# Seven products of quarter blocks for eight in the down projections of three feed-forward stages

## The chip, the cores and the metric

The kernel runs on one core of a Trainium2 chip. Its metric is the device time in microseconds (us) of one execution of the whole program, the median of three runs. A profiled execution is recorded besides, and every duration in this text comes from that one.

Five engines work side by side, each through its own queue of instructions in order: TensorE multiplies matrices (PE in the profile, its weight loads PEld), VectorE (DVE) and ScalarE (ACT) work element by element, GpSimd (POOL) too, and SyncE (SP) issues most transfers. An instruction starts when its predecessor on its engine lets it and when the semaphores it waits for have been raised by the others.

## The reference

The reference is a transformer block with a mixture of experts, followed by a second block of two layers. Each of these layers holds two feed-forward stages, four in all, which are the part that matters here:

```
D_MODEL = 1024; SEQ = 512; D_FF = 2816; FFN_HALF = 0.5

def swiglu(h, w_gate, w_up, w_down):
    return (jax.nn.silu(h @ w_gate) * (h @ w_up)) @ w_down

for i in range(DEPTH_2):                                   # 2 layers
    h = rmsnorm_2(x, ffn1_norm[i])
    x = x + FFN_HALF * swiglu(h, ffn1_w_gate[i], ffn1_w_up[i], ffn1_w_down[i])
    ...                                                    # layer 0: pooling mixer, layer 1: latent attention
    h = rmsnorm_2(x, ffn2_norm[i])
    x = x + FFN_HALF * swiglu(h, ffn2_w_gate[i], ffn2_w_up[i], ffn2_w_down[i])
```

In order of time: ffn1 of layer 0, pooling, ffn2 of layer 0, ffn1 of layer 1, attention, ffn2 of layer 1.

## The kernel before

All products are made in float32 by three passes. An operand is split into a high part (`hi`, rounded to the type fp32r in which TensorE multiplies at full rate) and the remainder (`lo` = operand - `hi`), and `mm3` (lines 246 to 249) adds hi·hi, hi·lo and lo·hi. ScalarE makes the high part with a cast, VectorE the remainder with a subtraction.

The residual stream `X` stays in SBUF: 512 tokens as 4 tiles of 128, 1024 features each. The normed input lies transposed in `xT`. The function `ffn` (line 1030) walks over the 22 blocks of 128 hidden features in three parts, `PARTS` (blocks 0 to 7, 8 to 14, 15 to 21). For each block it makes gate and up, 24 matmuls of 128x512 each, into one of two tiles `pA`; ScalarE takes Silu of the gate (L1052), VectorE multiplies by the up half (L1054), and the hidden block is split into `hh`, `hl` (L255, L256). At the end of a part comes its down projection, in two halves of 512 output features: four accumulators (2 `pB`, 2 `pC`, one for each token tile), and for each block 4 x 3 matmuls of 128x512. When an accumulator is done, VectorE adds half of it onto `X` (L1103).

The class `Weights` feeds the weights. A plan lists, in the order of their use, chunks of 1 MB (one DMA into one of 4 `wraw` tiles) and units (pieces of a chunk of up to 128x1024). `next()` hands out a split unit and lets the splitting run ahead by `look` = 2 units: ScalarE casts `whi` (L161) and VectorE subtracts to `wlo` (L162). There are `NU` = 4 buffers of `whi` and of `wlo`. A chunk's tile is free when its last unit is split, and then the next DMA is issued.

What order the instructions have in each queue is decided when the program is built, by a scheduler with its own estimate of readiness and by priorities (`tc.high_priority`); on the chip each queue then runs in that order.

Of the kernel before, what the change touches and what calls it, by code (L numbers as in the profile page):

```python
# [99 lines left out]
class Weights:  # L100
# [51 lines left out]
    def _split(self, i):  # L152
        c, pick, raw = self.units[i]
        src = pick(self.tiles[c])
# [36 lines left out]
def tile_net(ctx, tc, I, out):  # L191
# [195 lines left out]

    PARTS = [(0, 8), (8, 15), (15, 22)]

    def plan_ffn(which, i):  # L390
        g, u, d = (I[f"ffn{which}_w_{n}_2"][i] for n in ("gate", "up", "down"))
        for f0, f1 in PARTS:
# [643 lines left out]

    def ffn(pool, gain, last=False, hook=None, before=None):
        xT = pair()
# [7 lines left out]
        def proj(a, m, w, c0, c1):  # L1046
            for k in range(K):
                mm3(a[:, m * 512 + c0:m * 512 + c1], [x[:, k] for x in w], [x[:, k, c0:c1] for x in xT], k == 0, k == K - 1)

        def hidden_of(a, m, sl):  # L1050
# [4 lines left out]
            hh = pool.tile([P, S], F32R, name="hh", tag="hh", bufs=8)  # L1055
            hl = pool.tile([P, S], F32R, name="hl", tag="hl", bufs=8)
            split(hh, hl, sl)
            return hh, hl

        for f0, f1 in PARTS:  # L1060
            if hook is not None and f0 > 0:
# [412 lines left out]
    with tc.tile_pool(name="pmc", reuse_waits=RW, bufs=1) as pmc:  # L1474
        with tc.tile_pool(name="f10", reuse_waits=RW, bufs=1) as p_:
# [11 lines left out]
    with tc.tile_pool(name="ml", reuse_waits=RW, bufs=1) as ml:  # L1487
        with tc.tile_pool(name="f20", reuse_waits=RW, bufs=1) as p_:
# [37 lines left out]
```

## Time and profile before

| | |
|---|---|
| three runs, median (lowest to highest) | 2657.82 us (2657.05 to 2658.94) |
| profiled execution, its own time | 2660.51 us |
| span of that profile, first to last instruction | 2658.6 us |
| mean granted TensorE clock | 0.989 of full speed |
| instructions | 28917, of which 12006 matmuls |
| HBM read | 407.92 MB, 154 GB/s over the span |

How to read it: an engine's share of the span tells only the average. Which engine bounds a stage is read from that stage's window, and what a removed instruction is worth from the pace at which that engine issues. Matmuls are pipelined: the duration of one is longer than the distance to the next. The same holds to a smaller degree for VectorE, where an instruction may start a little before the one ahead of it has ended.

### The profile page before, as it was taken

How to read it: one execution, taken by the hardware profiler on the slowest of the kernel's cores; microseconds unless marked ns; L12 is line 12 of the kernel's file. 1: busy time of each engine (PE TensorE's matmuls, PEld its weight loads, DVE VectorE, ACT ScalarE, POOL GpSimd, SP SyncE). 2: the span in 40 equal slices, each digit the busy share in tenths (PEclk: the TensorE clock that was granted, in tenths of full speed). 3: DMA queues.
4: the chain of work that ended last, by engine and by line, in shares of the span. 5: the costliest groups of instructions: out<-in, count | busy, mean ns of one | idle time of the engine just before them, and what ended most of it. 6: DMA issues, size and time to landing. Idle time of an engine off the chain costs nothing.

```text
span 2658.6 us, 28917 instructions
## 1 busy us (share of the span) xinstructions
PE 2552.4 (96%) x12006; PEld 1856.7 (70%) x12006; DVE 1045.2 (39%) x1620; ACT 735.8 (28%) x1243; POOL 88.2 (3%) x142
## 2 busy tenths in 40 slices
PE   6999889999998999998999999999999999999999
PEld 4755644333335887888887878787779777888887
DVE  5655322222215333336333334333335666533332
ACT  4343210000003322224322223222224645322221
POOL 1000100000001000001000000000001000000000
PEclk9999899999998999999999999999999999999999
DMA  7255369999996222332222223223222111232321
GB/s 266 92 178 172 145 278 420 410 418 419 417 420 242 96 95 87 95 103 83 95 96 87 87 95 104 95 79 103 78 89 80 58 58 64 64 99 75 119 77 59
DMA packets 185493, 411.90 MB, mean 155 GB/s; under 512 B 7461, under 2 KB 126785, under 8 KB 157713
## 3 DMA queue, kind: packets, MB, share of 16 engines
q1 hardware_dynamic: 183168, 403.73, 41.6%
q10 hardware_dynamic: 1008, 3.34, 0.3%
q0 software_dynamic: 1184, 2.97, 0.3%
q8 instruction: 94, 1.54, 0.2%
q14 instruction: 39, 0.31, 0.0%
HBM read 407.92 MB, written 2.10 MB: 154 GB/s over the span
## 4 chain that ended last, share of the span: by engine, by line
PE 60%; issue 30%; DMA 3%; DVE 3%; ACT 3%; POOL 1%; SPq 0%; POOLq 0%; ACTq 0%; DVEq 0%
PE pA L968 9%; PE pA L247 7%; PE pA L248 7%; PE pA L249 7%; PE pB L968 4%; PE pC L249 3%; PE pC L248 3%; PE pC L247 3%; PE pB L248 2%; PE pB L249 2%; PE pB L247 2%; PE pC L942 1%; PE ms L1397 1%; PE pC L1015 1%; PE pC L741 1%
## 5 line engine op out<-in xcount | busy, mean ns | idle before, releaser
L161 ACT CAST whi<-wraw 128x1024 fp32r<-128x1024 f32 (+2 forms) x334 | 335.9, 1011 | 1093.7 <-PE pA L248 685.8
L162 DVE TENSOR_TENSOR wlo<-wraw,whi 128x1024 fp32r<-128x1024 f32 (+2 forms) x334 | 392.0, 1177 | 481.7 <-ACT whi L161 470.3
L248 PE MATMUL pA<-xTl,whi 128*128 128x512 f32 (+1 forms) x1536 | 578.1, 377 | 1.6 <-DVE xTl L256 1.6
L249 PE MATMUL pA<-xTh,wlo 128*128 128x512 f32 (+1 forms) x1536 | 578.2, 377 | 0.0
L247 PE MATMUL pA<-xTh,whi 128*128 128x512 f32 (+1 forms) x1536 | 574.0, 381 | 1.5 <-ACT xTh L255 1.3
L247 PEld LDWEIGHTS pA<-xTh,whi 128*128 128x128 f32 x1536 | 289.8, 189 | 76.8 <-ACT sl L1052 21.7
L249 PEld LDWEIGHTS pA<-xTh,wlo 128*128 128x128 f32 x1536 | 289.9, 189 | 56.6
L248 PEld LDWEIGHTS pA<-xTl,whi 128*128 128x128 f32 x1536 | 290.1, 189 | 55.2 <-DVE xTl L256 2.1
L1054 DVE TENSOR_TENSOR sl<-pA,sl 128x512 f32<-128x512 f32 x88 | 60.8, 691 | 427.6 <-PE pA L249 427.6
L968 PE MATMUL pA<-wraw,wideh 128*64 128x512 f32 x736 | 201.9, 597 | 1.4 <-DMA wraw<-in_w_up_dram 0.9
L247 PE MATMUL pC<-whi,hh 128*128 128x512 f32 x352 | 138.4, 393 | 0.0
L249 PE MATMUL pC<-whi,hl 128*128 128x512 f32 x352 | 138.4, 393 | 0.0
L248 PE MATMUL pC<-wlo,hh 128*128 128x512 f32 x352 | 138.4, 393 | 0.0
L247 PE MATMUL pB<-whi,hh 128*128 128x512 f32 x352 | 138.2, 393 | 0.0
L248 PE MATMUL pB<-wlo,hh 128*128 128x512 f32 x352 | 138.1, 392 | 0.0
L249 PE MATMUL pB<-whi,hl 128*128 128x512 f32 x352 | 138.1, 392 | 0.0
L968 PEld LDWEIGHTS pA<-wraw,wideh 128*64 128x64 f32 x736 | 58.2, 136 | 92.2 <-issue 88.5
L968 PE MATMUL pB<-wraw,hx 128*64 128x512 f32 x344 | 101.2, 597 | 1.0 <-DMA wraw<-in_w_down_dram 1.0
L247 PEld LDWEIGHTS pB<-whi,hh 128*128 128x128 f32 x352 | 66.1, 188 | 15.5 <-DVE X L1103 0.7
L249 PEld LDWEIGHTS pB<-whi,hl 128*128 128x128 f32 x352 | 66.1, 188 | 14.9
L247 PEld LDWEIGHTS pC<-whi,hh 128*128 128x128 f32 x352 | 66.1, 188 | 14.9
L248 PEld LDWEIGHTS pB<-wlo,hh 128*128 128x128 f32 x352 | 66.1, 188 | 14.7
(495 smaller groups left out, 3290.2 us busy)
## 6 DMA issues: line engine op xcount, KB each, us to landing
wraw<-in_w_gate_dram SPq DMA_DIRECT2D x47, 1024.0 KB, 14.0
wraw<-in_w_up_dram SPq DMA_DIRECT2D x45, 1024.0 KB, 10.7
wraw<-in_w_down_dram SPq DMA_DIRECT2D x43, 1024.0 KB, 11.1
wraw<-in_ffn_w_gate_dram SPq DMA_DIRECT2D x40, 1024.0 KB, 5.3
wraw<-in_ffn_w_up_dram SPq DMA_DIRECT2D x40, 1024.0 KB, 5.3
wraw<-in_ffn_w_down_dram SPq DMA_DIRECT2D x32, 1024.0 KB, 4.9
wraw<-in_w_ada_dram SPq DMA_DIRECT2D x24, 1024.0 KB, 7.9
widel<-in_w_up_dram SPq DMA_DIRECT2D x14, 1024.0 KB, 11.5
```

Of the source, the lines that this page charges most:

```text
L161: self.nc.scalar.copy(out=hi, in_=src)
L162: self.nc.vector.tensor_sub(lo, src, f(hi))
L247: PE.matmul(o, a[0], b[0], start=first, stop=False)
L248: PE.matmul(o, a[0], b[1], start=False, stop=False)
L249: PE.matmul(o, a[1], b[0], start=False, stop=last)
L741: PE.matmul(o[r], Vf[:, blk, r], x, start=z == 0, stop=z == len(blks) - 1)
L942: PE.matmul(p, ohr[:, t], h[:, t, c_], start=t + z == 0, stop=t + z == T)
L968: PE.matmul(outs[dh][r], x[:, k, r], ws[e][:, j, dh * 512:(dh + 1) * 512], start=k == 0, stop=k == K - 1)
L1015: PE.matmul(p, Se[:, t * P:(t + 1) * P], ys[dh][s], start=s == 0, stop=s == 1)
L1054: V.tensor_mul(sl, a[:, 512:1024], sl)
L1397: PE.matmul(p[:, :nn], q[a][:, c_], k[b][:, :nn], start=first, stop=False)
```

## The change

Of the four feed-forward stages, all but the first get a new down projection. Their 22 hidden blocks are walked in four parts, 0 to 5, 6 to 11, 12 to 17 and 18 to 21. The last part keeps the old way. In each of the others the six blocks are taken as three pairs, and for each pair the product of hidden block (512 tokens x 256) and weights (256 x 1024) is a 2 x 2 block product: quarters of 256 tokens x 128 on one side, 128 x 512 on the other. Strassen's seven products replace the eight. In what follows such a part's seven products are called a Strassen stage; there are nine of them in the program.

Each product needs sums or differences of quarters on both sides, and they are made before the split. On the hidden side `turn_pair` makes seven operands from a pair's `hr` (two blocks in one tile), five by an addition on VectorE. On the weight side `_split_sums` lets GpSimd add or subtract two quarters into a buffer `wsum` (two buffers), and ScalarE and VectorE split that sum; five of the seven products need it, two take a plain quarter. One product's units are one of two pairs (128x1024 in two halves) and one of one pair (128x512). Each product is accumulated over the three pairs in two banks (`pB` and `pC` in turn), and `add` puts the banks on one or two quarters of `X`.

```diff
+    def _split_sums(self, i, parts):
+        n = len(parts)
+        hi = self.sp.tile([P, 1024], F32R, name="whi", tag="whi")[:, :n * 512].rearrange("p (a b) -> p a b", b=512)
+        lo = self.sp.tile([P, 1024], F32R, name="wlo", tag="wlo")[:, :n * 512].rearrange("p (a b) -> p a b", b=512)
+        if parts[0][2] is None:
+            for j, (c, pick, _, _) in enumerate(parts):
+                self.nc.scalar.copy(out=hi[:, j], in_=pick(self.tiles[c]))
+                self.nc.vector.tensor_sub(lo[:, j], pick(self.tiles[c]), f(hi[:, j]))
+        else:
+            for j, (c, a, b, op) in enumerate(parts):
+                t = self.tmp.tile([P, 512], F32, name="wsum", tag="wsum", bufs=2)
+                self.nc.gpsimd.tensor_tensor(out=t, in0=a(self.tiles[c]), in1=b(self.tiles[c]), op=op)
+                self.nc.scalar.copy(out=hi[:, j], in_=t)
+                self.nc.vector.tensor_sub(lo[:, j], t, f(hi[:, j]))
...
     PARTS = [(0, 8), (8, 15), (15, 22)]
+    FAST = [(0, 6), (6, 12), (12, 18), (18, 22)]
+    PRODUCTS = [(0, (0, 0), (1, 1), OP.add), (2, (0, 1), (1, 1), OP.subtract), (6, (1, 0), (1, 1), OP.add),
+                (5, (0, 0), (0, 1), OP.add), (1, (0, 0), None, None), (3, (1, 0), (0, 0), OP.subtract),
+                (4, (1, 1), None, None)]
...
+            cs = [chunk([(0, P, rows(d, fa * P, 2, 0, D))], (P, 2, D)) for fa in range(f0, f1, 2)]
+            for _, a, b, op in PRODUCTS:
+                for z in range(0, len(cs), 2):
+                    W.sums([(c, quarter(a), quarter(b), op) for c in cs[z:z + 2]])
...
+        if fast:
+            W.tmp = pool
+            W.open_ring(3, pool, 1)
...
+        def turn_pair(hs, hr):
+            a11, a21, a12, a22 = hr[:, 0, 0:256], hr[:, 0, 256:512], hr[:, 1, 0:256], hr[:, 1, 256:512]
+            hi, lo = operand("shi"), operand("slo")
+            split(hi[:, 2], lo[:, 2], a11)
+            split(hi[:, 3], lo[:, 3], a22)
+            h = [pool.tile([P, 3, 256], F32, name="hq", tag="hq", bufs=1)]
+            V.tensor_add(h[0][:, 0], a11, a22)
+            V.tensor_add(h[0][:, 1], a21, a22)
+            split(hi[:, 0:2], lo[:, 0:2], h[0][:, 0:2])
+            h.append(pool.tile([P, 3, 256], F32, name="hq", tag="hq", bufs=1))
+            V.tensor_add(h[1][:, 0], a11, a12)
+            V.tensor_sub(h[1][:, 1], a21, a11)
+            V.tensor_sub(h[1][:, 2], a12, a22)
+            split(hi[:, 4:7], lo[:, 4:7], h[1])
+            hs.append((hi, lo))
...
+        def strassen(hs, n):
+            def product(i, banks):
+                m = PRODUCTS[i][0]
+                ws = [W.next() for _ in range((n + 1) // 2)]
+                for g in range(2):
+                    for z in range(n):
+                        mm3(banks[g], [x[:, m, g * P:(g + 1) * P] for x in hs[z]], [x[:, z % 2] for x in ws[z // 2]],
+                            z == 0, z == n - 1)
+            def add(banks, half, dh, sign=0.5):
+                for g in range(2):
+                    x = X[:, 2 * half + g, dh * 512:(dh + 1) * 512]
+                    V.scalar_tensor_tensor(x, banks[g], sign, x, op0=OP.mult, op1=OP.add)
+            for i, goes in enumerate((((1, 1, 1), (0, 0, 1)), ((0, 1, 1), (1, 1, 1)), ((0, 0, 1),), ((1, 1, 1),),
+                                      ((1, 0, 1), (1, 1, -1)), ((0, 0, 1), (1, 0, 1)), ((0, 0, -1), (0, 1, 1)))):
+                b = [psC(), psC()] if i % 2 else [psB(), psB()]
+                product(i, b)
+                for half, dh, sign in goes:
+                    add(b, half, dh, 0.5 * sign)
...
-            ffn(p_, nxt, hook=lambda: pcs.extend(pool_consts(pmc, p_)), before=final_norm)
+            ffn(p_, nxt, hook=lambda: pcs.extend(pool_consts(pmc, p_)), before=final_norm, fast=False)
```

Every fifth chunk of these stages goes to a fifth `wraw` tile (ring 3), and a pair of hidden blocks shares one tile `hr` with one buffer.

VectorE's queue in the down projection of a middle part of the second feed-forward stage, in the kernel before; `X` is the residual, `wlo` the weights' remainders:

```order
L1103 SCALAR_TENSOR_TENSOR X_71<-pB_8809,X_71 128x512
L162 TENSOR_TENSOR wlo_8926<-wraw_8712,whi_8925 128x1024
L1103 SCALAR_TENSOR_TENSOR X_71<-pB_8810,X_71 128x512
L1103 SCALAR_TENSOR_TENSOR X_71<-pC_8811,X_71 128x512
L1103 SCALAR_TENSOR_TENSOR X_71<-pC_8812,X_71 128x512
L162 TENSOR_TENSOR wlo_8954<-wraw_8712,whi_8953 128x512
```

And in the middle of a Strassen stage now, from the fourth product's weights to the fifth's; `wsum` is GpSimd's sum:

```order
L188 TENSOR_TENSOR wlo_8770<-wsum_8771,whi_8769 128x512
L188 TENSOR_TENSOR wlo_8770<-wsum_8775,whi_8769 128x512
L1176 SCALAR_TENSOR_TENSOR X_71<-pB_8767,X_71 128x512
L188 TENSOR_TENSOR wlo_8780<-wsum_8781,whi_8779 128x512
L1176 SCALAR_TENSOR_TENSOR X_71<-pB_8768,X_71 128x512
L182 TENSOR_TENSOR wlo_8808<-wraw_8296,whi_8807 128x512
L182 TENSOR_TENSOR wlo_8808<-wraw_8405,whi_8807 128x512
L182 TENSOR_TENSOR wlo_8814<-wraw_8436,whi_8813 128x512
L1176 SCALAR_TENSOR_TENSOR X_71<-pC_8805,X_71 128x512
L1176 SCALAR_TENSOR_TENSOR X_71<-pC_8806,X_71 128x512
```

The remainders of the next product's weights now stand between the additions of the previous one's banks, one queue for both.

GpSimd's queue at the same place before; it had the norms' small instructions alone, and between the second and the third row lies a whole feed-forward stage:

```order
L262 TENSOR_SCALAR ms_7387<-ss_7385 128x1
L263 TENSOR_TENSOR rstd_7388<-ms_7387,mhalf_87 128x1
L262 TENSOR_SCALAR ms_9726<-ss_9724 128x1
L263 TENSOR_TENSOR rstd_9727<-ms_9726,mhalf_87 128x1
L262 TENSOR_SCALAR ms_9749<-ss_9747 128x1
```

And now, from the third product's first sum on:

```order
L186 TENSOR_TENSOR wsum_8731<-wraw_8296 128x512
L186 TENSOR_TENSOR wsum_8735<-wraw_8405 128x512
L186 TENSOR_TENSOR wsum_8741<-wraw_8436 128x512
L186 TENSOR_TENSOR wsum_8771<-wraw_8296 128x512
L186 TENSOR_TENSOR wsum_8775<-wraw_8405 128x512
L186 TENSOR_TENSOR wsum_8781<-wraw_8436 128x512
L186 TENSOR_TENSOR wsum_8841<-wraw_8296 128x512
L186 TENSOR_TENSOR wsum_8845<-wraw_8405 128x512
L186 TENSOR_TENSOR wsum_8851<-wraw_8436 128x512
```

Fifteen sums a stage now stand there; each reads two quarters of a weight chunk.

## Rows read from the trace of the kernel before

**Rows 1.** The page's first part: busy us, share of the span, instructions.

```profile
PE 2552.4 (96%) x12006; PEld 1856.7 (70%) x12006; DVE 1045.2 (39%) x1620; ACT 735.8 (28%) x1243; POOL 88.2 (3%) x142
```

**Rows 2.** Windows over the three stages: us, engines' busy us, clock, DMA.

```profile
core 0: us, PE busy (x) PEld busy (x) DVE busy (x) ACT busy (x) POOL busy (x), PEclk, DMA share, GB/s
1250.00:1625.00 375.00, 373.13 (x1701) 301.78 (x1699) 134.95 (x176) 99.33 (x126) 2.62 (x7) 1.00 0.27 89
1630.00:2010.00 380.00, 377.90 (x1721) 306.21 (x1720) 136.69 (x152) 101.42 (x129) 4.16 (x10) 1.00 0.29 94
2290.00:2658.00 368.00, 364.39 (x1649) 296.98 (x1647) 120.78 (x133) 90.69 (x109) 0.00 (x0) 1.00 0.26 86
```

**Rows 3.** VectorE in order of time, first and second half of one down projection.

```profile
start us, us, engine line op out<-in xcount [idle before <-releaser]
957.32 1.37 DVE L1103 SCALAR_TENSOR_TENSOR X<-pB,X 128x512 f32<-128x512 f32 x2 [1.05 <-PE pB L249]
...
979.08 1.37 DVE L1103 SCALAR_TENSOR_TENSOR X<-pB,X 128x512 f32<-128x512 f32 x2 [1.09 <-PE pB L249]
```

**Rows 4.** Groups by line, shapes apart: count, busy us, mean ns, idle before.

```profile
L162 DVE TENSOR_TENSOR wlo<-wraw,whi 128x1024 fp32r<-128x1024 f32 x294 | 358.9, 1224 | 463.7 <-ACT whi L161 452.5 <-PE pB L623 4.1
...
L162 DVE TENSOR_TENSOR wlo<-wraw,whi 128x768 fp32r<-128x768 f32 x20 | 18.9, 953 | 8.4 <-ACT whi L161 8.2
...
L162 DVE TENSOR_TENSOR wlo<-wraw,whi 128x512 fp32r<-128x512 f32 x16 | 10.9, 681 | 0.0
...
L1103 DVE SCALAR_TENSOR_TENSOR X<-pB,X 128x512 f32<-128x512 f32 x48 | 33.0, 689 | 70.9 <-PE pB L249 70.9
...
L161 ACT CAST whi<-wraw 128x512 fp32r<-128x512 f32 x16 | 9.9, 621 | 59.0 <-PE pA L248 45.6 <-PE pC L249 13.3
```

**Rows 5.** VectorE in order of time, 829 to 834 and 2056 to 2058.

```profile
829.83 0.69 DVE L1017 TENSOR_TENSOR X<-pC,X 128x512 f32<-128x512 f32 x1 [0.23 <-PE pC L1015]
830.44 1.21 DVE L162 TENSOR_TENSOR wlo<-wraw,whi 128x1024 fp32r<-128x1024 f32 x1
831.57 1.28 DVE L282 SCALAR_TENSOR_TENSOR hrow<-X,rstd,gain 128x1024 f32<-128x1024 f32 x1
833.29 1.28 DVE L1478 SCALAR_TENSOR_TENSOR X<-X,rstd,gain 128x1024 f32<-128x1024 f32 x1 [0.44 <-POOL rstd L263]
...
2056.76 0.41 DVE L256 TENSOR_TENSOR cTl<-pC,cTh 128x256 fp32r<-128x256 f32 x1
2057.09 0.41 DVE L256 TENSOR_TENSOR cTl<-pB,cTh 128x256 fp32r<-128x256 f32 x1
```

**Rows 6.** TensorE in order of time, two matmuls of a gate projection.

```profile
994.00 0.39 PE L249 MATMUL pA<-xTh,wlo 128*128 128x512 f32 x1
994.23 0.39 PE L247 MATMUL pA<-xTh,whi 128*128 128x512 f32 x1
```

**Rows 7.** GpSimd in order of time, at 294, 326 and 826 to 834.

```profile
294.43 1.67 POOL L850 TENSOR_TENSOR X<-X,tmp 128x512 f32<-128x512 f32 x1 [28.24 <-DVE tmp L849]
...
325.96 2.34 POOL L883 TENSOR_TENSOR h2l<-got,h2h 128x1024 fp32r<-128x1024 f32 x1 [8.98 <-ACT got L882]
...
826.13 0.19 POOL L262 TENSOR_SCALAR ms<-ss 128x1 f32<-128x1 f32 x1 [487.04 <-ACT junk L275]
...
830.28 0.56 POOL L263 TENSOR_TENSOR rstd<-ms,mhalf 128x1 f32<-128x1 f32 x1
831.19 0.51 POOL L262 TENSOR_SCALAR ms<-ss 128x1 f32<-128x1 f32 x1 [0.35 <-ACT junk L275]
831.78 1.47 POOL L263 TENSOR_TENSOR rstd<-ms,mhalf 128x1 f32<-128x1 f32 x1
```

**Rows 8.** VectorE in order of time, beside GpSimd's addition at 294.

```profile
294.26 0.68 DVE L850 TENSOR_TENSOR X<-X,tmp 128x512 f32<-128x512 f32 x1
```

**Rows 9.** The page's sixth part: count, KB each, us to landing.

```profile
wraw<-in_ffn_w_gate_dram SPq DMA_DIRECT2D x40, 1024.0 KB, 5.3
```

**Rows 10.** Windows of the pooling mixer and the attention.

```profile
1215.00:1229.00 14.00, 8.87 (x68) 8.01 (x66) 12.18 (x11) 8.34 (x11) 2.02 (x2) 0.97 0.54 174
1228.20:1235.00 6.80, 6.02 (x27) 5.64 (x26) 5.56 (x9) 3.81 (x8) 0.00 (x0) 0.50 0.67 226
2165.00:2180.00 15.00, 13.30 (x77) 11.27 (x76) 10.34 (x21) 11.88 (x37) 2.03 (x2) 1.00 0.19 72
```

More of the change, by code (lines that the diff above doesn't have):

```diff
@@ L120, in unit, with sums @@
         self.left[c] += 1
+    def sums(self, parts):
+        self.units.append((max(p[0] for p in parts), parts, 0))
+        for p in parts:
+            self.left[p[0]] += 1
     def open_ring(self, ring, pool, bufs):
@@ L388, in tile_net, with quarter, plan_fast, chunk @@
     PARTS = [(0, 8), (8, 15), (15, 22)]
+    FAST = [(0, 6), (6, 12), (12, 18), (18, 22)]
+    PRODUCTS = [(0, (0, 0), (1, 1), OP.add), (2, (0, 1), (1, 1), OP.subtract), (6, (1, 0), (1, 1), OP.add),
+                (5, (0, 0), (0, 1), OP.add), (1, (0, 0), None, None), (3, (1, 0), (0, 0), OP.subtract),
+                (4, (1, 1), None, None)]
+    def quarter(q):
+        return q and (lambda v: v[:, q[0], q[1] * 512:q[1] * 512 + 512])
+    def plan_fast(which, i):
+        g, u, d = (I[f"ffn{which}_w_{n}_2"][i] for n in ("gate", "up", "down"))
+        nth = 0
+        def chunk(srcs, shape):
+            nonlocal nth
+            nth += 1
+            return W.chunk(srcs, shape, ring=3 if nth % 5 == 0 else 0)
+        for f0, f1 in FAST:
+            for fa in range(f0, f1, 2):
+                cs = [chunk([(0, P, rows(ap, 0, K, fa * P, 2 * P))], (P, K, 2 * P)) for ap in (g, u)]
+                for a in range(2):
+                    for c in cs:
+                        W.unit(c, lambda v, a=a: v[:, :, a * P:(a + 1) * P])
+            if f1 == FB:
+                for dh in range(2):
+                    c = chunk([(0, P, rows(d, f0 * P, 4, dh * 512, 512))], (P, 4, 512))
+                    for k in (0, 2):
+                        W.unit(c, lambda v, k=k: v[:, k:k + 2])
+                continue
+            cs = [chunk([(0, P, rows(d, fa * P, 2, 0, D))], (P, 2, D)) for fa in range(f0, f1, 2)]
+            for _, a, b, op in PRODUCTS:
+                for z in range(0, len(cs), 2):
+                    W.sums([(c, quarter(a), quarter(b), op) for c in cs[z:z + 2]])
     def plan_ffn(which, i):
+        if (which, i) != (1, 0):
+            plan_fast(which, i)
+            return
         g, u, d = (I[f"ffn{which}_w_{n}_2"][i] for n in ("gate", "up", "down"))
@@ L1034, in tile_net, with ffn @@
     W.sp = ctx.enter_context(tc.tile_pool(name="wsp1", reuse_waits=RW, bufs=NU))
-    def ffn(pool, gain, last=False, hook=None, before=None):
+    def ffn(pool, gain, last=False, hook=None, before=None, fast=True):
         xT = pair()
@@ L1054, in hidden_of, with new_sl @@
             V.tensor_mul(sl, a[:, 512:1024], sl)
-            hh = pool.tile([P, S], F32R, name="hh", tag="hh", bufs=8)
-            hl = pool.tile([P, S], F32R, name="hl", tag="hl", bufs=8)
+            if fast and not final:
+                return None
+            if fast:
+                if len(hs) % 2 == 0:
+                    halves[:] = [operand(z).rearrange("p a b -> p (a b)") for z in ("shi", "slo")]
+                hh, hl = (x[:, len(hs) % 2 * S:len(hs) % 2 * S + S] for x in halves)
+            else:
+                hh, hl = (pool.tile([P, S], F32R, name=z, tag=z, bufs=8) for z in ("hh", "hl"))
             split(hh, hl, sl)
             return hh, hl
-        for f0, f1 in PARTS:
+        def new_sl(fb):
+            if not fast:
+                return pool.tile([P, S], F32, name="sl", tag="sl", bufs=2)
+            if fb % 2 == 0:
+                hrs[:] = [pool.tile([P, 2, S], F32, name="hr", tag="hr", bufs=1)]
+            return hrs[0][:, fb % 2]
+        def strassen(hs, n):
[16 more added lines that the diff above has]
+                    add(b, half, dh, 0.5 * sign)
+        hrs = []
+        for f0, f1 in FAST if fast else PARTS:
+            final = f1 == FB
             if hook is not None and f0 > 0:
@@ L1081, in ffn @@
                 a = psA()
-                sl = pool.tile([P, S], F32, name="sl", tag="sl", bufs=2)
+                sl = new_sl(fb)
                 for m in range(2):
@@ L1085, in ffn @@
                     r = hidden_of(a, m, sl)
-                hs.append(r)
+                if r:
+                    hs.append(r)
+                elif fb % 2:
+                    turn_pair(hs, hrs[0])
             n = f1 - f0
+            if fast and not final:
+                strassen(hs, n // 2)
+                continue
             for dh in range(2):
@@ L1493, in tile_net @@
             ffn(p_, nxt)
+        W.room[3] = 0
         nxt, gain = gain, load_gain(I["ffn2_norm_2"][1:2])
```

16 lines of the change are left out of this document (14 added, 2 removed).

## The prediction, made before the changed kernel ran

> **What bounds the kernel now.** I read the page's first part, then the windows of the three stages that change. TensorE holds 96% of the span [rows 1], and in these stages 99% (1115.4 of 1123.0 us) at full clock, while VectorE has 35%, ScalarE 26% and GpSimd under 1% [rows 2]. So there a matmul that goes is worth the distance at which TensorE issues. Two rows give it: the additions of one down projection begin at 957.32 us and those of its other half, 96 matmuls later, at 979.08 [rows 3], that is 21.76 / 96 = 0.2267 us. The other engines have room on average; whether they have it in the stretch into which the new work is packed is the question.
>
> **What goes.** A Strassen stage has 7 products x 2 banks x 3 pairs x 3 passes = 126 matmuls where the old way had 6 blocks x 24 = 144. That is 18 x 0.2267 = 4.08 us a stage, and 9 stages make 36.7 us.
>
> **What comes, in one stage.** I take the stretch from the last up matmul of a part to the first gate matmul of the next. Five matmuls of the first product stand ahead of that last up projection, so 121 are left in it, 27.4 us of TensorE. The kernel before needs 144 - 5 = 139 there, 31.5 us. A stage gains as long as its stretch is shorter than 31.5 us.
>
> VectorE's queue in this stretch, counted in the order of the changed program: 16 remainders of weights, 20 additions onto X, one multiplication and one hidden remainder, all 128x512; six pieces of 128x256; one of 128x768. Durations of the same forms are 681 and 689 ns for 512 and 953 ns for 768 [rows 4]. Back to back they stand closer than they last: 830.44 - 829.83 = 0.61 (0.605 from duration less 0.08), 2057.09 - 2056.76 = 0.33 for 256 [rows 5], and 0.87 for 768 by the same 0.08. So 38 x 0.605 + 6 x 0.33 + 0.87 = 25.8 us. It begins 0.44 after the last up matmul: a matmul's result is there 0.39 to 0.40 after its start [rows 6], and a hand-over takes 0.04 (a norm's factor ends at 831.78 + 1.47, its reader starts at 833.29 [rows 5, 7]). The queue's next entry is the remainder of the next gate's weights, 1.22 [rows 4] and a hand-over, 1.26; TensorE can start two matmuls, 0.45, before it needs that. The stretch is then 0.44 + 25.8 + 1.26 - 0.45 = 27.1 us plus every microsecond W in which VectorE waits. TensorE needs 27.4. So from here on VectorE's queue sets the stage, and W up to 4.4 us is free of loss against the old way.
>
> W comes from GpSimd. A sum is 1.15 us: half of the 2.34 of the 128x1024 subtraction, and the addition of 294.43 lasted 1.67 of which 0.51 went by until VectorE's own addition, 294.26 + 0.68, had ended [rows 7, 8]. That is the point on which the case turns. GpSimd's small instructions show the same: 0.19 alone, 0.51 when VectorE subtracts the weights' remainder (until 831.65), and 0.55 alone, 1.47 when VectorE reads X and the gain (until 832.85) [rows 5, 7]. In each the instruction ended when VectorE's, with two inputs in SBUF, had. Beside an addition with one input in PSUM (829.83 to 830.52) GpSimd's at 830.28 kept its 0.56. So remainders and sums take turns, additions onto X take no part. The trace shows only GpSimd in the waiting role. What a sum in progress does to a remainder lies between nothing and the whole 1.15 plus the 0.08 of overlap lost; I take the whole, because GpSimd, too, got nothing done while it waited.
>
> Here the Trainium skill speaks (SBUF — State Buffer, Who interferes with whom): a VectorE instruction with two SBUF inputs and a GpSimd instruction that reads SBUF exclude each other, and whichever starts first keeps the port for its whole length. GpSimd's half of this agrees with the 1.47 for 0.55 above; VectorE's half no row here shows. By the whole rule the sum is the forecast's, by the half shown it is the first rival's.
>
> With it I followed the stage row by row, each step starting at the latest of its queue's pace, its inputs plus 0.04, and the end of the other engine's turn; times from the last up matmul. A sum's buffer is free when the remainder two sums earlier has been read, and the cast between is 0.62 [rows 4].
> - Third product's second and third sum run 2.06 to 3.21 and 5.16 to 6.31, the fourth's first 6.99 to 8.14. Each came ahead of a hidden-side piece of VectorE and cost it 1.15 + 0.08 = 1.23: together 3.7.
> - The fourth product's last sum is kept out by two remainders back to back until 16.76; then sum to 17.91, cast to 18.57, while the next sum has its turn from 17.99 to 19.14. VectorE, free at 17.28, waits 1.86.
> - The sixth product's second sum, 19.86 to 21.01, costs VectorE, free at 20.35, 0.66.
> - The sixth product's last sum, again behind two remainders, 25.33 to 26.48, cast to 27.14: VectorE, free at 25.86, waits 1.32.
>
> W = 3.7 + 1.86 + 0.66 + 1.32 = 7.5, the stretch 34.6 us, 3.1 more than before. Nine stages: +28 us.
>
> The rest is small. Making a pair's seven operands adds 3.8 us to VectorE (seven of 256, one of 512, one of 768) and drops two remainders; per pair TensorE works 96 x 0.23 [rows 6] = 22 us and VectorE then 9.6 (four remainders at 1.14, two products at 0.6, the 3.8), so it is hidden; `hr` has one buffer, and the next Silu comes 24 matmuls, 5.5 us, later, which covers the 3.8; without that cover it would be up to 1 us a pair. The last part is now four blocks: a token tile is done every 12 matmuls, 2.7 us, instead of 21, while its addition, norm (1.28 [rows 5], 1.2 without overlap) and two remainders keep VectorE 0.6 + 1.2 + 1.2 = 3.0; at the two changed boundaries 0 to 2.4 us in all, I take 1. The three down tiles stay occupied for a stage, so the second gate and up chunks are issued only at its end; they land 5.3 us after issue [rows 9], one behind the other, and are wanted 22 later: nothing.
>
> The sum: 2660.5 (profiled execution) + 28 + 1 = 2689.5. The median of the runs is 2.7 below that execution, so 2687 us.
>
> **Rivals.** First: GpSimd waits for VectorE, never the other way. For it speaks that a remainder began at 830.44, in time, inside GpSimd's 830.28 to 830.84 [rows 5, 7]; against it, that this reads one column. W is then the late sums alone: one of the third product 1.9, the fourth and the sixth 1.3 each, 0.2 of small ones: 4.7. Stretch 31.8, +0.3 each: 2660.5 + 3 + 1 - 2.7 = 2662 us.
>
> Second, on the other side, faster: sums and remainders don't hinder each other at all, the long durations at 294 and 831 having another cause. W falls to 0.8 + 0.8 + 0.4 = 2.0, the stretch to 29.1, -2.4 each, -21 us: 2637 us. It decides from W below 4.4. The three instructions of GpSimd that wait out VectorE's, at 294.43, 831.19 and 831.78 [rows 7], speak against it; that I may have set VectorE's queue too slow speaks for it.
>
> Third: as forecast, and TensorE's clock falls. In the forecast TensorE works 27.4 of 34.6 us, 79%, with waits up to 2.2 us. After a stretch in which it was busy 8.9 of 14 us, the granted clock fell to 0.50 (1.2 GHz) for 6.8 us; through one of 13.3 of 15 us it stayed at 1.00 (2.4 GHz) [rows 10]. The rows don't tell with which of them our stretch goes. If each stage lost half of such a 6.8 us, it is 9 x 3.4 = 31 more: 2718 us.
>
> **How the numbers follow.** Forecast 0.55, its own range 2672 to 2703 (W 1.7 lower or higher per stage); first rival 0.15; second 0.17; third 0.13. The range 2638 to 2712 leaves out about half of the second and two thirds of the third rival, under 2 in 10. About 0.2%, 5 us, is what a measurement can tell from no change. Faster: the second rival, a third of the first and a sliver of the forecast, 0.23. Within 0.2%: 0.4 of the first and a little of the forecast, 0.08. Slower: 0.69.
>
> **What would show it.** In the changed profile, a stretch of some 34 to 35 us between the last up and the next gate matmuls, TensorE waiting for VectorE in it, VectorE busy for 26 of it; remainders that start only when a sum on GpSimd has ended, and sums with 1.7 us or more instead of 1.15. With stretches under 31.5 the forecast is wrong, and with remainders that begin while a sum runs its step on turns is. A longer gate and up stretch, or a clock below 1.00 in these stages, would be costs that I set at nothing.

## The result and the profile after

| | before | after |
|---|---|---|
| median, lowest to highest | 2658.38 us, 2657.05 to 2663.73 (4 runs) | 2681.21 us, 2679.93 to 2683.56 (4 runs) |
| span of the profile | 2658.6 us | 2680.0 us |
| TensorE's instructions | 12006 | 11844 |

After to before is 1.0079, interval 1.0067 to 1.0092: 0.8% slower, where +1.1% had been forecast (2687 us). The page's first part after, against [rows 1]:

```profile
PE 2534.7 (95%) x11844; PEld 1821.5 (68%) x11844; DVE 1332.4 (50%) x2106; ACT 810.3 (30%) x1426; POOL 292.2 (11%) x277
```

There are 162 matmuls less, 9 x 18, and TensorE's busy time fell only from 2552.4 to 2534.7 us. VectorE and GpSimd have 287 and 204 us more. The first of the stages that change, as a window, against the first row of [rows 2]:

```profile
1250.00:1625.00 375.00, 359.80 (x1604) 284.85 (x1603) 221.78 (x301) 119.42 (x177) 68.24 (x46) 1.00 0.26 89
```

TensorE is busy 96% in place of 99%: the time that the missing matmuls left became idle time, and more came to it. Nearly all of it lies in nine stretches, from a part's last up matmul to the next gate matmul. The second one, TensorE in order of time (last column: idle time before, and who ended it):

```profile
1424.14 0.40 PE L276 MATMUL pA<-xTh,wlo 128*128 128x512 f32 x1
...
1428.69 0.50 PE L274 MATMUL pB<-whi,shi 128*128 128x512 f32 x1 [0.67 <-ACT shi L282]
1430.96 0.73 PE L276 MATMUL pB<-whi,slo 128*128 128x512 f32 x2 [1.07 <-DVE slo L283]
1435.73 0.50 PE L274 MATMUL pB<-whi,shi 128*128 128x512 f32 x1 [1.71 <-DVE X L1176]
...
1458.46 0.40 PE L274 MATMUL pA<-xTh,whi 128*128 128x512 f32 x1
```

The stretch is 1458.46 - 1424.14 = 34.32 us (forecast: 34.6); the nine lie between 34.04 and 34.46, mean 34.26. TensorE waits for VectorE, and for casts behind it. What VectorE did there, and under it GpSimd, in order of time:

```profile
1426.12 1.53 DVE L1131 TENSOR_TENSOR hq<-hr 128x256 f32<-128x256 f32 x1
1427.58 0.41 DVE L1132 TENSOR_TENSOR hq<-hr 128x256 f32<-128x256 f32 x1
1427.91 1.28 DVE L188 TENSOR_TENSOR wlo<-wsum,whi 128x512 fp32r<-128x512 f32 x2
1429.11 1.79 DVE L283 TENSOR_TENSOR slo<-hq,shi 128x512 fp32r<-128x512 f32 x1
1430.94 1.40 DVE L1135 TENSOR_TENSOR hq<-hr 128x256 f32<-128x256 f32 x1
...
1436.79 2.47 DVE L1176 SCALAR_TENSOR_TENSOR X<-pC,X 128x512 f32<-128x512 f32 x4
...
1442.32 1.13 DVE L188 TENSOR_TENSOR wlo<-wsum,whi 128x512 fp32r<-128x512 f32 x1 [1.26 <-ACT whi L187]
...
1443.97 2.62 DVE L182 TENSOR_TENSOR wlo<-wraw,whi 128x512 fp32r<-128x512 f32 x3
...
1450.85 0.69 DVE L188 TENSOR_TENSOR wlo<-wsum,whi 128x512 fp32r<-128x512 f32 x1 [1.26 <-ACT whi L187]
```

```profile
1425.94 1.43 POOL L186 TENSOR_TENSOR wsum<-wraw 128x512 f32<-128x512 f32 x1 [3.76 <-DVE wlo L188]
1428.67 3.39 POOL L186 TENSOR_TENSOR wsum<-wraw 128x512 f32<-128x512 f32 x2 [1.30 <-DVE wlo L188]
1437.01 1.31 POOL L186 TENSOR_TENSOR wsum<-wraw 128x512 f32<-128x512 f32 x1 [4.96 <-DVE wlo L188]
1439.94 2.96 POOL L186 TENSOR_TENSOR wsum<-wraw 128x512 f32<-128x512 f32 x2 [1.62 <-DVE wlo L188]
1443.53 1.31 POOL L186 TENSOR_TENSOR wsum<-wraw 128x512 f32<-128x512 f32 x1 [0.63 <-DVE wlo L188]
1448.47 1.70 POOL L186 TENSOR_TENSOR wsum<-wraw 128x512 f32<-128x512 f32 x1 [3.63 <-DVE wlo L188]
```

This is the way a turn looks in such a trace: not as idle time of VectorE, but as an instruction that lasts too long. A 128x256 piece takes 0.41 us where it is left alone (1427.58) and 1.53 and 1.40 where a sum had started before it. The 128x512 remainder at 1429.11 takes 1.79 in place of 0.68. Beside them the four additions onto X run 2.47 us through the whole sum of 1437.01, neither longer than usual. And GpSimd waits the other way round: two sums that alone take 1.3 each needed 3.39 and 2.96.

### The profile page after: what moved, and what is told of

Its sections match the earlier page's. It is cut to its first block, busy times and chain, and to the rows that moved or that the text cites. A ratio compares the mean times of both kernels' runs of the same rounds, so it can differ in the third digit from the quotient of the medians.

```text
span 2680.0 us, 29534 instructions
## 1 busy us (share of the span) xinstructions
PE 2534.7 (95%) x11844; PEld 1821.5 (68%) x11844; DVE 1332.4 (50%) x2106; ACT 810.3 (30%) x1426; POOL 292.2 (11%) x277
## 3 DMA queue, kind: packets, MB, share of 16 engines
q8 instruction: 93, 1.52, 0.2%
## 4 chain that ended last, share of the span: by engine, by line
PE 64%; issue 17%; DVE 10%; ACT 3%; DMA 3%; POOL 2%; POOLq 0%; DVEq 0%; SPq 0%; ACTq 0%
PE pA L274 10%; PE pA L275 9%; PE pA L276 9%; PE pA L1033 8%; PE pB L1033 4%; PE pC L275 2%; PE pC L276 2%; DVE X L1176 2%; PE pC L274 2%; DVE wlo L188 1%; PE pB L275 1%; DVE slo L283 1%; PE pB L274 1%; PE pC L1007 1%; PE pB L276 1%
## 5 line engine op out<-in xcount | busy, mean ns | idle before, releaser
L171 DVE TENSOR_TENSOR wlo<-wraw,whi 128x1024 fp32r<-128x1024 f32 (+2 forms) x274 | 325.9, 1198 | 248.9 <-ACT whi L170 240.0
L186 POOL TENSOR_TENSOR wsum<-wraw 128x512 f32<-128x512 f32 x135 | 204.4, 1522 | 702.0 <-DVE wlo L188 437.4
L187 ACT CAST whi<-wsum 128x512 fp32r<-128x512 f32 x135 | 81.9, 619 | 274.9 <-PE pA L275 124.5
L274 PE MATMUL pB<-whi,shi 128*128 128x512 f32 x264 | 106.5, 403 | 20.2 <-DVE X L1176 14.0
L188 DVE TENSOR_TENSOR wlo<-wsum,whi 128x512 fp32r<-128x512 f32 x135 | 101.5, 773 | 43.3 <-ACT whi L187 43.3
L276 PE MATMUL pB<-whi,slo 128*128 128x512 f32 x264 | 104.5, 402 | 9.6 <-DVE slo L283 9.6
L275 PE MATMUL pB<-wlo,shi 128*128 128x512 f32 x264 | 105.0, 398 | 0.0
L275 PE MATMUL pC<-wlo,shi 128*128 128x512 f32 x210 | 85.2, 406 | 3.4 <-DVE wlo L188 3.3
L274 PE MATMUL pC<-whi,shi 128*128 128x512 f32 x210 | 83.3, 404 | 2.6 <-ACT whi L187 2.6
L276 PE MATMUL pC<-whi,slo 128*128 128x512 f32 x210 | 83.3, 397 | 0.0
```

What stands on the lines that cost most here:

```text
L186: self.nc.gpsimd.tensor_tensor(out=t, in0=a(self.tiles[c]), in1=b(self.tiles[c]), op=op)
L187: self.nc.scalar.copy(out=hi[:, j], in_=t)
L188: self.nc.vector.tensor_sub(lo[:, j], t, f(hi[:, j]))
L274: PE.matmul(o, a[0], b[0], start=first, stop=False)
L275: PE.matmul(o, a[0], b[1], start=False, stop=False)
L276: PE.matmul(o, a[1], b[0], start=False, stop=last)
```

## Experiments

Stretches are given as means over the nine. In runs 2, 9 and 11 the program's order leaves 16 matmuls of the last product to be done behind the next part's first gate matmul, so the stretch ends earlier by them; 3.7 us (16 x 0.2333, the pace below) are added there to make them comparable, and that is said. Ratios are to the kernel before, run on the same chip.

**1. No sums.** 

> Left out: the 54 sums of weight quarters on GpSimd; each remainder and each upper half is taken from the first quarter alone, straight from the loaded block. TensorE, ScalarE and VectorE have the same instructions as in the changed kernel. Theory (GpSimd's sums hinder VectorE, by turns and by waits, 6.9 us of each stretch): a stretch falls from 34.3 us to VectorE's own queue, 27 to 28.5 us, and the kernel from 2681 to 2615 to 2635 us, under the kernel before. Rival (VectorE's own queue of additions, splits and updates is too long by itself, GpSimd only goes along): the stretch stays over 32 us and the kernel over 2660 us.

```diff
-                self.nc.gpsimd.tensor_tensor(out=t, in0=a(self.tiles[c]), in1=b(self.tiles[c]), op=op)
-                self.nc.scalar.copy(out=hi[:, j], in_=t)
-                self.nc.vector.tensor_sub(lo[:, j], t, f(hi[:, j]))
+                self.nc.scalar.copy(out=hi[:, j], in_=a(self.tiles[c]))
+                self.nc.vector.tensor_sub(lo[:, j], a(self.tiles[c]), f(hi[:, j]))
```

Measured: 2635.72 us, ratio 0.9907 (0.9892 to 0.9922), stretch 29.50 us. So GpSimd's sums (15 in each of nine stages, 135 in all, not the 54 written down) cost 34.26 - 29.50 = 4.8 us a stretch, and without that cost the seven products would gain. The stretch is 1 us longer than the top of its range, and the kernel 0.7 us: here TensorE, not VectorE, sets the end. It works without a wait from the third product on, and ahead of the last three of the fifth product's additions it is VectorE that waits, 0.96 us for TensorE. The order of VectorE's queue shifts in places in this run; in run 3 it does not.

**2. The sums on VectorE.** 

> The same sums, but on VectorE. Theory: a sum on GpSimd costs VectorE more than doing it itself. Eight sums of 0.605 us are 4.8 us in a stretch, against 6.9 us of hindrance that goes: the stretch is 31.5 to 32.5 us, the kernel 2655 to 2668 us, faster than the changed kernel, about level with the one before. Rival (GpSimd's work is beside VectorE's, and only late once or twice): VectorE's queue grows by most of 4.8 us in nine stretches, 2700 to 2725 us.

```diff
-                self.nc.gpsimd.tensor_tensor(out=t, ...)
+                self.nc.vector.tensor_tensor(out=t, ...)
```

Measured: 2662.98 us, 1.0013 (1.0004 to 1.0023), stretch 28.33 + 3.7 = 32.1. As the theory had it: doing all the work in one queue is faster than dividing it between two engines that keep each other out. VectorE now works without a gap, and every piece has its undisturbed length again.

**3. GpSimd only writes.** 

> GpSimd writes each sum's buffer with a constant and reads nothing (the sums' values are left out); the order, the buffers and the waits between GpSimd, ScalarE and VectorE stay. Theory (turns: VectorE's two-input remainders stand still while GpSimd reads): the remainders and splits fall back to 0.68 and 0.41 us, only the waits for a buffer or for the upper half are left; the stretch is 28 to 30 us, the kernel 2625 to 2645 us. Rival (the chain sum, upper half, remainder is late, whatever GpSimd reads): a shorter operation shortens it a little, but most of it stays: stretch over 32 us, kernel over 2660 us. Rival (any write of GpSimd's stops VectorE as well): the long durations stay.

```diff
-                self.nc.gpsimd.tensor_tensor(out=t, ...)
+                self.nc.gpsimd.memset(t, 0.5)
```

Measured: 2638.22 us, 0.9918 (0.9903 to 0.9933), stretch 29.55, the same as without sums. Groups by line, shapes apart:

```profile
L188 DVE TENSOR_TENSOR wlo<-wsum,whi 128x512 fp32r<-128x512 f32 x135 | 89.7, 687 | 22.6 <-ACT whi L187 21.1
L186 POOL MEMSET wsum<- 128x512 f32 x135 | 71.1, 527 | 787.5 <-DVE wlo L188 784.9
L283 DVE TENSOR_TENSOR slo<-hq,shi 128x512 fp32r<-128x512 f32 x27 | 18.5, 685 | 0.0
```

The last row's remainder of the hidden side had 1172 ns on the mean in the changed kernel:

```profile
L283 DVE TENSOR_TENSOR slo<-hq,shi 128x512 fp32r<-128x512 f32 x27 | 31.6, 1172 | 0.0
```

The buffers and the order of VectorE's, ScalarE's and TensorE's queues are the changed kernel's, instruction for instruction, and the long durations are gone, so the second rival falls too. But 0.53 us is also less time than a sum's 1.3, so length and reading are not yet told apart.

**4. Seven buffers in the last stage.** 

> Seven buffers for sums in place of two in the last feed-forward stage alone (the two others have no room), so GpSimd can work ahead of VectorE's remainders. If half of the loss is lateness (the waits of 1.26 us for the upper half behind a late sum, two a stretch), the three last stretches fall from 34.05 us to 30 to 32 us and the kernel to 2669 to 2675 us; sums that run earlier, in the gate and up part, take their turns where VectorE has room. If all of it is turns at the same places, or the sums wait for the weights to land, nothing changes: 2678 to 2682 us.

```diff
-                t = self.tmp.tile([P, 512], F32, name="wsum", tag="wsum", bufs=2)
+                t = self.tmp.tile([P, 512], F32, name="wsum", tag="wsum", bufs=self.sums_ahead)   # 7 if last else 2
```

Measured: 2677.01 us, 1.0063 (1.0048 to 1.0078). The three last stretches fell from 34.07 to 32.08 us, each 2.0 less; stretch and kernel end just outside the ranges given for lateness, and far from those for turns alone. The middle one as a window, then the same stretch in the changed kernel; the last number in brackets counts GpSimd's instructions:

```profile
2471.83:2503.91 32.08, 28.58 (x124) 22.67 (x122) 30.98 (x47) 13.27 (x22) 4.77 (x3) 1.00 0.14 44
```

```profile
2472.20:2506.27 34.07, 29.78 (x124) 22.35 (x122) 31.13 (x46) 13.48 (x22) 11.93 (x8) 1.00 0.10 32
```

Five of the eight sums now run before the stretch, none of the rest comes late, and the two waits of 1.26 us are gone: 2.0 us less. Three sums are left in it. With seven buffers they are the sixth product's, but they start where the third product's second and third sum and the fourth's first had started, and VectorE's pieces there last 1.52, 1.76 and 1.39 us, as before (1.53, 1.79, 1.40). From 29.0 us (run 5, these three stretches) to 32.1 these turns cost the rest, 3.1 us. So the loss has two parts: turns at the start, and sums that come late because VectorE kept GpSimd out.

**5. GpSimd writes twice.** 

> As the run in which GpSimd only writes (the sums' values are left out), but it writes each buffer twice, 2 x 0.527 us, so that it is occupied nearly as long as with a sum (1.15 to 1.3 us alone). It tells length from reading. Theory (turns: VectorE's instructions with two inputs in SBUF stand still while GpSimd reads SBUF): no reading, no turns, VectorE's durations stay 0.68 and 0.41 us and the stretch stays at 29.5 to 30.3 us, the kernel at 2636 to 2645 us. Rival (a late chain of sum, upper half, remainder, by GpSimd's time alone): the waits for the upper half come back, the stretch goes to 32 to 34 us, the kernel to 2660 to 2680 us.

```diff
-                self.nc.gpsimd.tensor_tensor(out=t, ...)
+                self.nc.gpsimd.memset(t, 0.5)
+                self.nc.gpsimd.memset(t, 0.5)
```

Measured: 2635.59 us, 0.9907 (0.9892 to 0.9922), stretch 29.40, both at the lower edge of the theory's ranges. GpSimd and VectorE in order of time, at the place where a sum had cost a piece 1.1 us:

```profile
1419.74 0.53 POOL L186 MEMSET wsum<- 128x512 f32 x1 [4.84 <-DVE wlo L189]
1420.32 0.53 POOL L187 MEMSET wsum<- 128x512 f32 x1
```

```profile
1419.93 0.42 DVE L1132 TENSOR_TENSOR hq<-hr 128x256 f32<-128x256 f32 x1
1420.27 0.42 DVE L1133 TENSOR_TENSOR hq<-hr 128x256 f32<-128x256 f32 x1
```

GpSimd is occupied for 1.1 us, and VectorE's pieces run through it at 0.42. Length alone costs nothing, and the waits of 1.26 us are gone too: a writing GpSimd is not kept out either. What costs is reading.

**6. GpSimd reads one quarter.** 

> GpSimd copies the first quarter into the sum's buffer in place of adding two (the sums' values are left out): one input read from SBUF. Theory (turns go with any reading of GpSimd's): remainders and splits on VectorE grow long again (over 1.1 us where they meet a copy), as in the changed kernel, by the copy's own length: with some 0.6 to 1.2 us for a copy the stretch is 30.5 to 33.5 us, the kernel 2645 to 2674 us. Rival (only GpSimd instructions with two inputs keep VectorE out): as with writing alone, 29.5 to 30.3 us and 2636 to 2645 us.

```diff
-                self.nc.gpsimd.tensor_tensor(out=t, ...)
+                self.nc.gpsimd.tensor_copy(out=t, in_=a(self.tiles[c]))
```

Measured: 2646.94 us, 0.9952 (0.9936 to 0.9967), stretch 30.46. The same places again, VectorE, then GpSimd:

```profile
1417.29 0.83 DVE L1131 TENSOR_TENSOR hq<-hr 128x256 f32<-128x256 f32 x1
...
1419.59 1.10 DVE L283 TENSOR_TENSOR slo<-hq,shi 128x512 fp32r<-128x512 f32 x1
1420.72 0.71 DVE L1135 TENSOR_TENSOR hq<-hr 128x256 f32<-128x256 f32 x1
```

```profile
1417.11 0.75 POOL L186 COPY wsum<-wraw 128x512 f32<-128x512 f32 x1 [5.16 <-DVE wlo L188]
1419.13 2.03 POOL L186 COPY wsum<-wraw 128x512 f32<-128x512 f32 x2 [1.27 <-DVE wlo L188]
```

One input is enough. Each of the three pieces is longer by 0.3 to 0.4 us where a copy (0.61 alone) had started before it, as it was by 1.1 and 1.0 with a sum. So the price of a turn went by how long GpSimd reads, in the two lengths tried.

**7. A shorter queue, all at once.** 

> All sums on VectorE, and its queue shortened without changing what is computed: a product goes into one two-bank tile and is added onto X by one instruction of 128x1024 in place of two of 512 (12 in place of 24 a stage), sums of two pairs share a buffer, an upper half and a remainder of 128x1024, and two pairs of 128x256 pieces become one piece each. By the rows a second instruction saved is 2 x 0.605 - 1.13 = 0.08 us: 10 + 4 + 2 of them in a stretch are 1.2 us. Theory (VectorE's queue is the bound with the sums on it, some 32 us in the count of the changed kernel): 30.5 to 31.5 us, the kernel 2646 to 2657 us, faster than the one before by 0.1 to 0.5%. Rival (the waits between the engines bound, not the queue: a wide addition starts only when both halves are done): no gain, 2660 to 2668 us.

```diff
-            for j, (c, a, b, op) in enumerate(parts):
-                t = self.tmp.tile([P, 512], F32, name="wsum", tag="wsum", bufs=2)
+            t = self.tmp.tile([P, 2, 512], F32, name="wsum", tag="wsum", bufs=1)[:, :n]
+            for j, (c, a, b, op) in enumerate(parts):
+                self.nc.vector.tensor_tensor(out=t[:, j], ...)
...
-                b = [psC(), psC()] if i % 2 else [psB(), psB()]
+                b = psA().rearrange("p (a b) -> p a b", b=512)
...
-                for g in range(2):
-                    V.scalar_tensor_tensor(x, banks[g], sign, x, op0=OP.mult, op1=OP.add)
+                V.scalar_tensor_tensor(x, banks, sign, x, op0=OP.mult, op1=OP.add)   # x: two token tiles
```

Measured: 2709.93 us, 1.0189 (1.0171 to 1.0208), stretch 37.4, a miss by some 58 us. Fewer and longer instructions made the waits longer: with one shared buffer and one cast for both, VectorE stands still between a pair of sums and its remainder.

```profile
1441.79 1.29 DVE L186 TENSOR_TENSOR wsum<-wraw 128x512 f32<-128x512 f32 x2
1444.27 1.22 DVE L188 TENSOR_TENSOR wlo<-wsum,whi 128x1024 fp32r<-128x1024 f32 x1 [1.19 <-ACT whi L187]
```

The next three runs take the bundle apart.

**8. Wide additions alone.** 

> Sums on VectorE in their two buffers of 128x512, as in the run with the sums on VectorE; only the additions onto X are 12 of 128x1024 in place of 24 of 128x512 a stage, for which a product goes into one two-bank tile, the tile that the gate and up projections use. Theory (VectorE's queue is the bound; a saved instruction is 0.08 us): 0.8 us less in a stretch, 2655 us (2650 to 2659). Rival (the two-bank tile, not the shared sum buffer, is what cost the bundled run its 47 us: a product waits until both halves of the last but one have been added): 2675 to 2710 us.

 The edit is the last two pieces of run 7's. Measured: 2690.02 us, 1.0108 (1.0094 to 1.0122), stretch 35.5: the rival's range, but not the rival's reason. In a stretch at full clock (34.98 us, the last row of this document), TensorE's longest wait for an addition onto X is 1.08 us; in run 2, with single banks, it is 1.21. What is new is that VectorE waits for ScalarE's casts. The split of 128x768 no longer has two additions ahead of it, and sums stand right ahead of their own remainders, with a cast between:

```profile
1818.37 0.96 DVE L283 TENSOR_TENSOR slo<-hq,shi 128x768 fp32r<-128x768 f32 x1 [0.90 <-ACT shi L282]
...
1837.38 0.69 DVE L186 TENSOR_TENSOR wsum<-wraw 128x512 f32<-128x512 f32 x1
1838.83 0.69 DVE L188 TENSOR_TENSOR wlo<-wsum,whi 128x512 fp32r<-128x512 f32 x1 [0.76 <-ACT whi L187]
```

With three more (0.17, 0.16 and 0.53) these waits are 2.5 us of the 2.8 by which this stretch is longer than run 2's; in run 2 VectorE has none of them. So most of the cost lies in the order in which the scheduler put VectorE's queue for the wide additions.

**9. Fused pieces alone.** 

> Sums on VectorE, additions onto X in single banks as in the changed kernel; of the six 128x256 pieces of the last pair's hidden operands two pairs become one piece of 128x512 each. Theory (VectorE's queue is the bound): two instructions saved, 0.16 us a stretch plus the same in each pair, which is hidden: 1 to 2 us, 2661 us (2657 to 2664). Rival (something else in the bundle costs): over 2668 us.

```diff
-            V.tensor_add(h[0][:, 0], a11, a22)
-            V.tensor_add(h[0][:, 1], a21, a22)
+            q = hr.rearrange("p a (b c) -> p (a b) c", c=256)
+            V.tensor_add(h[0][:, 0:2], q[:, 0:2], q[:, 3:4].to_broadcast([P, 2, 256]))
...
-            V.tensor_sub(h[1][:, 1], a21, a11)
-            V.tensor_sub(h[1][:, 2], a12, a22)
+            V.tensor_sub(h[1][:, 1:3], q[:, 1:3], q[:, 0:4:3])
```

Measured: 2659.96 us, 1.0000 (0.9991 to 1.0009), stretch 28.06 + 3.7 = 31.8, 0.3 under run 2's, inside the theory's range; level with the kernel before.

**10. Both.** 

> Both of the two others together, sums in two buffers of 128x512. Theory: 1 us less in a stretch than with the sums on VectorE alone, 2653 us (2648 to 2658), 0.1 to 0.4% under the kernel before. Rival (the two-bank tile costs): 2675 to 2710 us.

 Measured: 2687.13 us, 1.0107 (1.0092 to 1.0122). Wide additions cost again, with VectorE's queue in the order of run 8 and the same waits for casts; no run has the two-bank tile in run 2's order. Run 7 is this run with a shared buffer, one cast and one remainder for a pair of sums: these took the ratio from 1.0107 to 1.0189, 0.8 points beside the 1.1 between run 9 and this one.

**11. Two sums where they fit.** 

> As the run with the fused pieces (all sums on VectorE), but the first two sums of the fourth product, which come right behind four additions onto X, go to GpSimd. Theory (an addition onto X has its bank in PSUM and takes no turns, so two sums of 1.27 us fit beside 2.4 us of additions): VectorE's queue is 1.2 us shorter and loses 0 to 0.5 us to a late pair, so 0.7 to 1.2 us a stretch less, 2649 to 2655 us, under the kernel before by 0.2 to 0.4%. Rival (a GpSimd sum costs VectorE more than 0.6 us wherever it stands): 2660 us or more.

```diff
+                (self.nc.gpsimd if i in self.aside else self.nc.vector).tensor_tensor(out=t, ...)
...
+                    W.sums([...], (m, z) == (5, 0))   # the fourth product's first unit
```

Measured: 2646.42 us, 0.9947 (0.9934 to 0.9959): faster than both kernels, 0.5% under the one before, and 3 us below the theory's range. Stretch 26.74 + 3.7 = 30.5, 1.3 less than run 9. VectorE, then GpSimd:

```profile
1423.53 0.68 DVE L1138 TENSOR_TENSOR hq<-hr 128x512 f32<-128x512 f32 x1
1424.13 1.28 DVE L1177 SCALAR_TENSOR_TENSOR X<-pB,X 128x512 f32<-128x512 f32 x2
1425.33 0.95 DVE L285 TENSOR_TENSOR slo<-hq,shi 128x768 fp32r<-128x768 f32 x1
...
1429.79 1.28 DVE L1177 SCALAR_TENSOR_TENSOR X<-pC,X 128x512 f32<-128x512 f32 x2
1430.99 1.66 DVE L190 TENSOR_TENSOR wlo<-wsum,whi 128x512 fp32r<-128x512 f32 x2
```

```profile
1423.40 1.98 POOL L188 TENSOR_TENSOR wsum<-wraw 128x512 f32<-128x512 f32 x1 [92.02 <-DVE wlo L190]
1429.95 1.32 POOL L188 TENSOR_TENSOR wsum<-wraw 128x512 f32<-128x512 f32 x1 [4.57 <-DVE wlo L190]
```

The first sum is kept out until the piece of 1423.53 has ended, and runs beside two additions onto X; nothing of VectorE's is longer. The second overlaps two additions and reaches 0.3 into the remainders (1.66 for 1.28). Together they took 1.2 us off VectorE's queue for 0.4. That is 0.8 of the 1.3 us; the stretch also goes by TensorE. In run 9 it waited at the fourth product:

```profile
1433.01 0.73 PE L274 MATMUL pC<-whi,shi 128*128 128x512 f32 x2 [1.05 <-ACT whi L187]
```

With 0.34 more a little later that is 1.39 us. In run 11 both waits are gone, and TensorE works without one from the third product to the end of the stretch: it is the bound again.

**12. A third sum.** 

> The same, and the third sum of the sixth product as well on GpSimd. Theory: at best 0.6 us a stretch more off VectorE's queue, 2644 to 2652 us; but there VectorE has remainders of weights on either side, so it may as well cost a turn of 1.2 us, 2655 to 2660 us. Rival as for the run with two: 2662 us or more.

 The edit is run 11's with `(m, z) in ((5, 0), (3, 2))`. Measured: 2654.45 us, 0.9974 (0.9964 to 0.9983), stretch 31.34, 0.9 more than run 11: just below the range of the second outcome named. The sum is issued while the second of two remainders runs on VectorE and lasts 1.64 for 1.3; its cast comes late, and VectorE waits:

```profile
1440.17 1.64 POOL L188 TENSOR_TENSOR wsum<-wraw 128x512 f32<-128x512 f32 x1 [9.32 <-issue]
```

```profile
1442.49 0.69 DVE L190 TENSOR_TENSOR wlo<-wsum,whi 128x512 fp32r<-128x512 f32 x1 [1.25 <-ACT whi L189]
```

## Why the prediction was right, and where it was off

**Turns.** The step on which the case turned holds, in both directions. [rows 5, 7] had shown only GpSimd waiting for VectorE; the rows after show VectorE waiting for GpSimd, for nearly the sum's whole length (0.99 to 1.12 of 1.3 us), and runs 3, 5 and 6 tie it to GpSimd's reading. The sentence of the Trainium skill (SBUF — State Buffer, Who interferes with whom) that named both directions agrees with these rows (1.53 for 0.41); the same section says that a GpSimd instruction which only writes does not collide with two SBUF inputs of VectorE's, and run 5 agrees (0.42 beside two writes). Two statements of the prediction do not hold as they were worded. Of the three GpSimd instructions that waited, only that of 831.19 ended when VectorE's did (831.70 against 831.65); those of 831.78 and 294.43 ended 0.40 and 1.16 us later, with work of their own still to do. And a remainder that begins while a sum runs was named as a sign against turns, VectorE busy for 26 us as one for them. The split of 1429.11 begins while GpSimd's two sums from 1428.67 on run, and VectorE is busy for 31.3 us. Both are turns all the same: the profile counts the waiting in the instruction's own duration, so the sign to look for is the length and not the start.

**W.** Forecast 7.5, measured 6.9 from the rows of the second stretch (forecasts in brackets): three turns of 1.12, 1.11 and 0.99 (3.7 in all), 1.26 at the fourth product's late sum with 0.45 more on the remainder behind it (1.86), 0.74 in the three plain remainders (0.66), 1.26 at the sixth product's late sum (1.32). The places are the ones followed row by row. A sum lasts 1.3 us alone, not the 1.15 worked out from [rows 7].

**VectorE's queue as the bound.** Right: 27.1 + 6.9 = 34.0 against 34.26 measured, and VectorE is busy for 31.33 of a stretch's 34.32 us (the windows under the last heading). With W gone TensorE is the next bound at 29.4 to 29.5 us (runs 1 and 5), not VectorE at 27.1 as the second rival's sum (27.1 + 2.0) had it. So removing GpSimd's reading gives 4.8 us a stretch and not 6.9. By run 4 it is the late sums whose cost was partly slack: 3.7 on VectorE, 2.0 in the stretch, while the three turns' 3.2 came through as 3.1.

**TensorE's pace: the term that was mis-sized.** 0.2267 us a matmul was taken from the additions of [rows 3], in the one feed-forward stage that does not change. In two of the three that do, the pace is slower. Two windows of the kernel before, the first in the second stage and the other in a down projection of the last, TensorE busy throughout, at full clock:

```profile
1280.00:1600.00 320.00, 320.00 (x1369) 255.45 (x1368) 105.53 (x115) 80.92 (x99) 0.00 (x0) 1.00 0.28 93
2376.00:2412.00 36.00, 36.00 (x160) 29.74 (x159) 12.51 (x13) 7.94 (x8) 0.00 (x0) 1.00 0.28 88
```

By the weight loads, 320 / 1368 = 0.234 and 36 / 159 = 0.226. The first window holds gate and up matmuls too, but the same work shows it as well: from the last up to the next gate matmul, the down projection of eight blocks took 42.18 us in the first stage (938.74 to 980.92) and 43.39 in the second (1342.38 to 1385.77), which is 0.2333 a matmul. The old way's stretch of 139 matmuls was thus 32.4 us in six stages and 31.5 in three, not 31.5 in all, and a stage lost 1.9 and 2.5 us, not 3.1: 19 in nine stages for the 28 forecast. From a stage's first gate matmul to its last down matmul, the three lost 6.3, 7.8 and 7.3, together the whole 21.4 us between the two spans. What the nine stretches leave of that is 2 to 3 us, nearly all of it in the third stage; at the boundaries 1 had been taken, and no run tells what the rest is. By medians the kernel lost 22.8 us, where 29 had been forecast: direction and mechanism are right, and the size was set about a quarter too large.

**The rivals.** The first (only GpSimd waits, 2662 us) falls with the long pieces of VectorE. The second (no hindrance, 2637 us) is what runs 3 and 5 show when the reading is taken away, 2638 and 2636 us, near its price but with TensorE as the bound. The third (a falling clock) did not decide: the mean clock is 0.989 in both kernels. The clock fell in two of the nine stretches, and these are as long as their neighbours; the rows at the end of this document show where such a dip costs.

**What was set at nothing** (making the pairs' operands, the later gate and up chunks): no loss beyond those 2 to 3 us, boundaries included, is left for them.

## What to carry to other kernels

Work given to GpSimd was not free for VectorE where GpSimd read SBUF and VectorE's instruction took both its inputs from there: price such a pair as one queue, and compare with doing it all on VectorE (here 32.1 us against 34.3). It was nearly free beside VectorE instructions that take an input from PSUM, and where the result isn't needed at once. With six of a stretch's eight sums moved to VectorE, two left so placed, and two pairs of small pieces fused, a loss of 0.8% became a gain of 0.5%. And take the pace of the bounding engine from the very stage that changes.

## What the runs showed that was not expected

TensorE's 128x512 matmuls have two paces at the same granted clock. The down projections of the first and the last feed-forward stage issue every 0.227 us; those of the two stages between, and the gate and up matmuls of all four, every 0.233. Why stays open; the share of the DMA engines is the same in both windows above.

A dip of the granted clock cost nothing where TensorE had a wait for VectorE behind it, and nearly its whole price where it had none. Two stretches of the changed kernel, the first with a dip of 3.4 us from 1.00 (2.4 GHz) to 0.50 (1.2 GHz); the last column but two is the mean granted clock:

```profile
1808.63:1842.95 34.32, 31.71 (x123) 23.54 (x122) 31.33 (x46) 13.57 (x22) 12.10 (x8) 0.95 0.10 32
1911.77:1946.09 34.32, 30.21 (x124) 22.38 (x122) 31.33 (x46) 13.49 (x22) 12.09 (x8) 1.00 0.10 31
```

TensorE works 1.5 us longer in the first, and its next wait for VectorE is shorter by about as much, 0.15 us where the same matmul waits 1.71 in the undisturbed stretch of 1424.14:

```profile
1820.21 0.50 PE L274 MATMUL pB<-whi,shi 128*128 128x512 f32 x1 [0.15 <-DVE X L1176]
```

And two of run 8's, the first with a dip as long, but 20 us into the stretch in place of 7. TensorE has no wait behind it to give up, the stretch is 1.6 us longer, and a remainder of VectorE's that waits 0.53 us for its cast in the other stretch waits 2.08:

```profile
1426.33:1462.87 36.54, 32.34 (x124) 23.61 (x122) 31.91 (x45) 13.39 (x22) 0.00 (x0) 0.95 0.10 32
1812.23:1847.21 34.98, 30.78 (x123) 22.44 (x122) 31.91 (x45) 13.39 (x22) 0.00 (x0) 1.00 0.11 33
```
